# The second projection of a ConvFFN by half-block sums: seven products for eight, with two of four weight sums per pair by accumulating DMAs and two on VectorE

## The chip, the cores and the metric

One Trainium2 chip, one core. The metric is the device time of one launch in microseconds. The kernel before takes 1299.2 us (median of three runs, 1298.52 to 1301.49). Engines: TensorE (PE, with PEld for its weight loads), VectorE (DVE), ScalarE (ACT), GpSimd (POOL), SyncE (SP, which issues DMAs).

## The reference

Two decoder layers in float32, batch 1, 512 positions (S), width 1024 (D). Layer 0 mixes with gated linear attention (GLA), layer 1 with gated DeltaNet (GDN); each is followed by a ConvFFN, and each sublayer ends in a LayerNorm over `ALPHA * h + f(h)`.

```python
def conv_ffn(x, w_in, conv_w, w_out):
    h = causal_dwconv(x @ w_in, conv_w)          # 1024 -> 2 x 2816, then width 3 in time
    gate, up = jnp.split(h, 2, axis=-1)
    return (jax.nn.gelu(gate, approximate=False) * up) @ w_out   # 2816 -> 1024

def reference(x, ...):
    h = x
    for i in range(2):
        y = gla_mixer(h, ...) if i == 0 else gdn_mixer(h, ...)
        h = layer_norm(ALPHA * h + y, ln_g[i, 0], ln_b[i, 0])
        h = layer_norm(ALPHA * h + conv_ffn(h, ffn_w_in[i], ffn_conv_w[i], ffn_w_out[i]),
                       ln_g[i, 1], ln_b[i, 1])
    return h
```

The change touches the last product of `conv_ffn`, (512 x 2816) by (2816 x 1024), in both layers.

## The kernel before

Float32 products are made of three products of split operands: a value is cast to a high part (fp32r, on ScalarE) and the rest is its low part (a subtraction on VectorE), and PE adds high by high, low by high and high by low in one PSUM bank. `split_out` does that for activations, `issue` for weights: SP loads 512 KB into one of three `raw` buffers, ScalarE casts it to `wh` (L243), VectorE subtracts to `wl` (L244). There are four `wh`/`wl` buffers (`WB`). `prefetch` issues items of the list `plan` a little ahead of their use (`look`); `weight()` takes the next, `spend()` gives its buffer back. The last `TAIL` = 4 items of an FFN go, as 512-wide halves, into slots of the common pool of 53 (`wsh`, L233, and `wsl`, L234), so that they need no `wh` buffer.

An FFN has 22 blocks of 128 hidden channels (`f`). They are worked in two chunks, of 12 and 10. In a chunk, `fm_items` runs the up-projection: per block a gate item and an up item of 24 products 128 x 512 each, into a bank `fm`; then `ffn_conv` (one operation on ScalarE, two on VectorE, L643), a GELU on ScalarE, the product of both on VectorE (L658) and the split into `gh` and `gl` (L417, L418), laid out as 128 channels by 512 positions. After that `out_proj` runs the output projection for the chunk: for each half `hf` of the 1024 columns `tm_half` goes over pairs of K blocks, and for each over the four token blocks `tb`, each with a bank `tm` of its own; after the last pair `done` adds the bank to the residual `h[tb][hf]` (L379 in the first chunk, with ALPHA; L381 in the second), in the last chunk takes statistics (L386) and, when both halves of a token block are there, starts the LayerNorm generator. That one normalizes (L527 to L552), transposes on PE (`xT`, L166) and splits into `xh` and `xl` for the next stage, or, in the last layer, scales, shifts and stores the output (L593 to L595).

The order of each engine is set when the program is built: a scheduler gives every instruction its place by the written order and by costs that the kernel counts up (`clk`, `vec`), and the engine then takes its list in order. The lists shown under the change are those.

Of the kernel before, what the change touches and what calls it, by code (L numbers as in the profile page):

```python
# [9 lines left out]
F32R = mybir.dt.float32r  # L10
# [3 lines left out]
ALU = mybir.AluOpType  # L14

P = 128
D = 1024
S = 512
# [11 lines left out]
GDN_SCALE = 128.0 ** -0.5  # L30
CHUNKS = ((0, 12), (12, 22))
SLOTS = 53
# [16 lines left out]
def blk(i, n=P):  # L49
    return slice(i * n, i * n + n)  # L50


class Trunk:
# [3 lines left out]
    def __init__(self, ctx, tc):  # L57
# [23 lines left out]
        self.plan = []  # L81
        self.issued = 0
        self.taken = 0
        self.held = 0
# [64 lines left out]

    def mm(self, out, a, b, start=True, stop=True):  # L150
        n = 1
        for d in b.shape[1:]:
            n *= d
        self.clk += n * (0.00045 if b.dtype == F32R else 0.00175)
        t = self.nc.tensor.matmul(out, a, b, start=start, stop=stop)  # L155
        if self.pin:
            self.tc.keep_in_program_order(t)
# [40 lines left out]
    @staticmethod  # L198
    def in_slots(item):
        return item[0] == "tm" and item[5]  # L200

    def issue(self, item):

        nc = self.nc
        if item[0] == "rep":
            return self.issue_rep(*item[1:])
        used = 1024
        raw = self.raw if self.issued == 0 else self.rp.tile([P, 1024], F32, name=self.uid("raw"), tag="raw")
# [52 lines left out]

    def prefetch(self):
        while self.issued < min(len(self.plan), self.taken + self.look):
            item = self.plan[self.issued]
            if self.held == WB and not self.in_slots(item):
                break
            if self.after is None:
                self.ready.append(self.issue(item))
            else:
                with self.tc.issue_after(self.after):  # L270
                    self.ready.append(self.issue(item))
                self.after = None
            self.issued += 1

    def weight(self):
# [94 lines left out]
    def out_proj(self, a, n, first, final):  # L370
# [25 lines left out]
        self.look = LOOKAHEAD  # L396


    def exp_ln_table(self):
# [223 lines left out]
    def ffn_plan(self, w_in, w_out):  # L623
        for f0, f1 in CHUNKS:
            for f in range(f0, f1):
                self.plan_fm(w_in, f * P)
                self.plan_fm(w_in, DFF + f * P)
            self.plan_out(w_out, f0 * P, f1 - f0, TAIL if f1 == NF else 0)

# [16 lines left out]
    def ffn(self, cw, li, g, b, final, out=False):  # L646
        nc = self.nc
        for ci, (f0, f1) in enumerate(CHUNKS):
            gs, act, items = [], {}, []
            for f in range(f0, f1):  # L650
                def gate(ps, f=f):
                    a = self.ffn_conv(ps, cw, f)
                    nc.scalar.activation(a, a, AF.Gelu)  # L653
                    act[f] = a

                def up(ps, f=f):
                    u = self.ffn_conv(ps, cw, NF + f)
                    nc.vector.tensor_mul(u, u, act.pop(f))  # L658
                    t = self.slot("gh", F32R), self.slot("gl", F32R)
                    self.split_out(*t, u)  # L660
                    gs.append(t)

                items += [gate, up]
            self.fm_items(items)
            last = ci == len(CHUNKS) - 1
            if last:
                self.drain()
                self.ln_begin(li, g, b)
                if out:
                    self.ln_gb()  # L670
            a = lambda c, tb: (gs[c][0][:, blk(tb)], gs[c][1][:, blk(tb)])
            self.out_proj(a, f1 - f0, ci == 0, final if last else None)

# [694 lines left out]
```

## Time and profile before

| view | value |
|---|---|
| median of three runs | 1299.2 us (1298.52 to 1301.49) |
| profiled execution, span | 1300.2 us |
| PE busy | 1279.0 us, 98% |
| VectorE busy | 790.2 us, 61% |
| ScalarE busy | 546.8 us, 42% |
| GpSimd busy | 111.0 us, 9% |
| DMA, mean over the span | 97 GB/s, 126.52 MB |

The span is that of one execution taken by the profiler; it stands 1.0 us above the median of the runs. The shares are means over the whole span. In the page each of the 40 slices stands for 32.5 us; PE shows a 9 in nearly all of them, and the granted clock of PE a 9 in all but two, in the GDN mixer.

### The profile page before, as it was taken

The numbers are of one execution on the slowest core, as the hardware profiler recorded it, in microseconds if no ns is written. First come the engines' busy times: TensorE is split into PE (matmuls) and PEld (weight loads), VectorE is DVE, ScalarE is ACT, GpSimd is POOL, SyncE is SP. The second block draws the span as 40 slices with busy tenths as digits, with TensorE's granted clock in tenths as the row PEclk, the third lists the DMA queues.
The fourth block names the chain that finished last, engine by engine and source line by source line (L and its number), as shares of the span: only waits on it lengthen the run. The fifth ranks groups of instructions, "written<-read, shape, count | busy, mean of one in ns | idle before, by whom it ended". The sixth has DMA issues, their size and how long they took to land.

```text
span 1300.2 us, 17238 instructions
## 1 busy us (share of the span) xinstructions
PE 1279.0 (98%) x6666; PEld 1078.1 (83%) x6666; DVE 790.2 (61%) x1442; ACT 546.8 (42%) x1030; POOL 111.0 (9%) x150
## 2 busy tenths in 40 slices
PE   8999999999999999999999999999999999999996
PEld 6878888988888888889788889988888888888885
DVE  3673366676643466655799835669677653366656
ACT  3554443634421344425865535543554431244420
POOL 4000000070000000001111310100034000000000
PEclk9999999999999999999999968999999999999999
DMA  6421224143333333251543420333143333333331
GB/s 181 117 81 49 77 86 130 33 130 114 98 97 97 97 97 98 87 143 66 135 117 106 127 49 17 115 98 113 49 137 107 97 98 98 97 97 97 97 98 65
DMA packets 167089, 126.52 MB, mean 97 GB/s; under 512 B 16088, under 2 KB 139546, under 8 KB 167008
## 3 DMA queue, kind: packets, MB, share of 16 engines
q1 hardware_dynamic: 161728, 115.10, 30.0%
q0 software_dynamic: 3888, 8.50, 2.1%
q10 hardware_dynamic: 1392, 1.84, 0.4%
q8 instruction: 52, 0.85, 0.3%
q14 instruction: 29, 0.24, 0.1%
HBM read 119.63 MB, written 5.78 MB: 96 GB/s over the span
## 4 chain that ended last, share of the span: by engine, by line
PE 86%; issue 6%; DVE 5%; DMA 1%; ACT 1%; POOL 1%; DVEq 0%; POOLq 0%; ACTq 0%
PE fm L155 45%; PE tm L155 32%; PE o L155 1%; PE V L155 1%; PE R L155 1%; PE xT L166 1%; PE vn L155 1%; DVE ln_st L386 1%; PE pg L155 1%; PE yT L166 1%; PE qkT L166 1%; PE pq L155 0%; DMA gla_nw<-in_gla_norm_w_dram 0%; DVE wl L244 0%; DVE conv L940 0%
## 5 line engine op out<-in xcount | busy, mean ns | idle before, releaser
L244 DVE TENSOR_TENSOR wl<-raw,wh 128x1024 fp32r<-128x1024 f32 (+1 forms) x190 | 238.3, 1255 | 321.1 <-ACT wh L243 319.3
L155 PE MATMUL fm<-xh,wh 128*128 128x512 f32 (+1 forms) x1104 | 408.3, 370 | 0.4 <-ACT wh L243 0.4
L155 PE MATMUL fm<-xl,wh 128*128 128x512 f32 (+1 forms) x1104 | 404.8, 367 | 0.0
L155 PE MATMUL fm<-xh,wl 128*128 128x512 f32 (+1 forms) x1096 | 401.2, 367 | 2.5 <-DVE wl L244 2.5
L243 ACT CAST wh<-raw 128x1024 fp32r<-128x1024 f32 (+1 forms) x190 | 198.8, 1047 | 269.9 <-PE tm L155 159.4
L155 PEld LDWEIGHTS fm<-xh,wl 128*128 128x128 f32 x1096 | 207.4, 190 | 36.5 <-DVE wl L244 3.1
L155 PEld LDWEIGHTS fm<-xh,wh 128*128 128x128 f32 x1104 | 209.1, 189 | 34.2 <-ACT wh L243 1.2
L155 PEld LDWEIGHTS fm<-xl,wh 128*128 128x128 f32 x1104 | 209.3, 190 | 32.7
L643 DVE SCALAR_TENSOR_TENSOR conv<-fm,ffn_cw,conv 128x511 f32<-128x511 f32 (+1 forms) x176 | 130.7, 745 | 3.0
L155 PE MATMUL tm<-wl,gh 128*128 128x512 f32 x288 | 112.0, 389 | 0.0
L155 PE MATMUL tm<-wh,gh 128*128 128x512 f32 x288 | 112.0, 389 | 0.0
L155 PE MATMUL tm<-wh,gl 128*128 128x512 f32 x288 | 112.0, 389 | 0.0
L155 PE MATMUL tm<-wh,xh 128*128 128x512 f32 x192 | 79.5, 414 | 1.0 <-ACT qk L756 1.0
L417 ACT CAST gh<-conv 128x512 fp32r<-128x512 f32 x44 | 27.3, 621 | 124.7 <-DVE conv L658 124.6
L155 PE MATMUL tm<-wh,xl 128*128 128x512 f32 x192 | 75.4, 393 | 0.0
L155 PE MATMUL tm<-wl,xh 128*128 128x512 f32 x192 | 75.1, 391 | 0.0
L653 ACT ACTIVATE conv<-conv 128x512 f32<-128x512 f32 x44 | 27.8, 633 | 95.0 <-DVE conv L643 95.0
L155 PEld LDWEIGHTS tm<-wh,gh 128*128 128x128 f32 x288 | 54.1, 188 | 11.2
L155 PEld LDWEIGHTS tm<-wh,gl 128*128 128x128 f32 x288 | 54.1, 188 | 11.2
L155 PEld LDWEIGHTS tm<-wl,gh 128*128 128x128 f32 x288 | 54.1, 188 | 11.2
L641 ACT ACTIVATE conv<-fm,ffn_cw 128x512 f32<-128x512 f32 x88 | 59.9, 681 | 0.2
L940 DVE SCALAR_TENSOR_TENSOR conv<-fm,gdn_cw,conv 128x509 f32<-128x509 f32 (+2 forms) x72 | 53.2, 742 | 4.6 <-ACT conv L938 4.1
(274 smaller groups left out, 1555.4 us busy)
## 6 DMA issues: line engine op xcount, KB each, us to landing
raw<-in_ffn_w_in_dram SPq DMA_DIRECT2D x88, 512.0 KB, 3.7
raw<-in_ffn_w_out_dram SPq DMA_DIRECT2D x44, 512.0 KB, 3.7
raw<-in_gdn_w_in_dram SPq DMA_DIRECT2D x32, 512.0 KB, 4.0
raw<-in_gla_w_in_dram SPq DMA_DIRECT2D x23, 512.0 KB, 3.5
raw<-in_gla_w_out_dram SPq DMA_DIRECT2D x8, 512.0 KB, 3.5
raw<-in_gdn_w_out_dram SPq DMA_DIRECT2D x8, 512.0 KB, 3.8
hd<-h POOLq DMA_DIRECT2D x8, 256.0 KB, 2.5
dt<-drow POOLq DMA_DIRECT2D x8, 256.0 KB, 5.6
```

Of the source, the lines that this page charges most:

```text
L155: t = self.nc.tensor.matmul(out, a, b, start=start, stop=stop)
L166: t = self.nc.tensor.transpose(out, a, self.ident[:n, :n])
L243: nc.scalar.copy(wh[:, cols], raw[:, cols])
L244: nc.vector.tensor_sub(wl[:, cols], raw[:, cols], wh[:, cols])
L386: nc.vector.bn_stats(self.st[tb][:, hf, :], h)
L417: cast = self.nc.scalar.copy(dst_h, src)
L641: nc.scalar.activation(a, ps, AF.Identity, scale=tap(2))
L643: nc.vector.scalar_tensor_tensor(a[:, d:], ps[:, :S - d], tap(2 - d), a[:, d:], ALU.mult, ALU.add)
L653: nc.scalar.activation(a, a, AF.Gelu)
L940: self.conv = nc.vector.scalar_tensor_tensor(a[:, d:], ps[:, :S - d], tap(3 - d), a[:, d:], ALU.mult, ALU.add)
```

## The change

The output projection of a chunk is worked on 2 x 2 blocks, by a scheme of seven half-size products in place of eight. For a pair of K blocks (e, o), the activations are cut in two halves of 256 positions and the weights in two halves of 512 columns: activations x11, x21 (from e), x12, x22 (from o), weights q00, q01 (rows of e) and q10, q11 (rows of o). `combine` makes, once per pair on VectorE, the four sums s1 to s4 of activation halves, at half width, and splits them and x11, x12 and x22 into high and low parts. `plan_sums` makes the weight side in `wq` slots by quadrants of 256 KB: a and b are loaded by SP; b becomes q01 + q00 by an accumulating DMA from GpSimd (L221); c is loaded as q11, b += c on VectorE (L224); c becomes q11 + q01 by a second accumulating DMA; a is loaded anew as q10, and b += a on VectorE. Each of these values is split to high and low when its product comes (`split_duo`: ScalarE L276, VectorE L277).

`sums_proj` runs the products: three kinds of bank, A, B and C, two each (one per 128 positions of a half). Bank A collects x11, then s2 is added on top, then s3, then x22, and after each it is added to or subtracted from a block of `h` (`fold`, L506 in the first touch of a block, L508 later, and L511 for the statistics); B collects s1, then s4; C collects x12. There are 14 folds per chunk where there were eight. The chunks are three, of 6, 8 and 8 blocks. A pair takes 7 x 2 x 3 = 42 products, where before it took 2 x 4 x 2 x 3 = 48. PE has 5540 rows in its list for 5672, VectorE 1672 for 1342, GpSimd 186 for 142.

```diff
-CHUNKS = ((0, 12), (12, 22))
+PAIRS = ((0, 3), (3, 7), (7, 11))
+HALF = 2 * P
+AHEAD = 2
...
+    def plan_sums(self, w, rows, last):
...
+        def load(t, i, r, col):
+            t[i] = self.slot("wq")
+            nc.sync.dma_start(t[i], quad(i, r, col))
+        def add(t, i, r, col):
+            nc.gpsimd.dma_start(t[i], quad(i, r, col), accum_op=ALU.add)
+        def plus(t, i, u):
+            nc.vector.tensor_add(t[i], t[i], u[i])
...
+        for i in range(n):
+            duo([(a, i), (b, i)], -1, False, (load, a, i, 0, 0), (load, b, i, 0, 1), (add, b, i, 0, 0))
+        for i in range(n):
+            duo([(b, i), (c, i)], base + i, False, (load, c, i, 1, 1), (plus, b, i, c))
...
+        if last:
+            twos(a, load, 1, 0)
+            twos(c, add, 0, 1, slots=True)
+        else:
+            for i in range(n):
+                duo([(c, i), (a, i)], base + n + i, False, (add, c, i, 0, 1), (load, a, i, 1, 0))
+        twos(b, plus, a, slots=last)
...
+    def sums_proj(self, xs, first, final):
...
+        def prod(bank, i, which, w, j, end):
...
+            self.mm(ps, xh, w[0], begin, False, True)
+            self.mm(ps, xh, w[1], False, False, True)
+            self.mm(ps, xl, w[0], False, end, True)
+        def fold(bank, j, tb, hf, op, full):
...
+                nc.vector.tensor_tensor(h, h, banks[bank][j], op)
...
+        pairwise((("A", "x11"), ("B", "s1")),
+                 (lambda j: (j, 0, add, False), lambda j: (2 + j, 1, add, False)))
+        pairwise((("A", "s2"), ("B", "s4")),
+                 (lambda j: (j, 1, sub, False), lambda j: (j, 1, add, True)))
+        if final is None:
+            pairwise((("A", "s3"), ("C", "x12")),
+                     (lambda j: (2 + j, 1, sub, False), lambda j: (j, 0, add, False)))
+        else:
...                                      # C x12 (done(0), done(1)), then A s3, each over all pairs
+        ws = [x for k in range(0, n, 2) for x in self.weight()]
+        for j in range(2):
+            for i in range(n):
+                prod("A", i, "x22", ws[i], j, i == n - 1)
+            fold("A", j, 2 + j, 0, add, True)
+            done(2 + j)
...
+    def combine(self, e, o):
...
+        nc.vector.tensor_sub(r[:, t0], e[:, t1], o[:, t1])
+        nc.vector.tensor_sub(r[:, t1], r[:, t0], e[:, t0])
+        self.split_out(x11[:, t0], x11[:, t1], e[:, t0])
+        x |= halves(r, ("s1", "s2"))
+        nc.vector.tensor_sub(d[:, t0], e[:, t0], e[:, t1])
+        nc.vector.tensor_add(d[:, t1], o[:, t0], r[:, t1])
+        x |= halves(d, ("s3", "s4"))
+        x |= halves(o, ("x12", "x22"))
```

Three places show how the instructions stand. The first is PE at the end of FFN 1, where the last output products (`tm`), the transposes of the normalized residual (`xT`; `h_97` and `h_98` are the two column halves of token block 1, `h_99` and `h_100` of block 2, `h_101` and `h_102` of block 3) and the first products of the GDN mixer (`fm`, 256 positions wide) meet. Before:

```order
L155 MATMUL tm_4451<-wsh_4478,gh_4274 128x512
L155 MATMUL tm_4451<-wsl_4479,gh_4274 128x512
L155 MATMUL tm_4451<-wsh_4478,gl_4275 128x512
L166 MATMUL xT_4735<-ident_80,h_99 128x128 x4
L166 MATMUL xT_4784<-ident_80,h_100 128x128 x4
L155 MATMUL fm_4796<-xh,wh_4484 128x256
L155 MATMUL fm_4796<-xl,wh_4484 128x256
```

Now:

```order
L158 MATMUL tm_4636<-wsh_4863,gl_4628 128x512
L169 MATMUL xT_5038<-ident_80,h_97 128x128 x4
L169 MATMUL xT_5087<-ident_80,h_98 128x128 x4
L169 MATMUL xT_5101<-ident_80,h_99 128x128 x4
L169 MATMUL xT_5113<-ident_80,h_100 128x128 x4
L169 MATMUL xT_5127<-ident_80,h_101 128x128 x4
L158 MATMUL fm_5139<-xh,wh_4919 128x256
L158 MATMUL fm_5139<-xl,wh_4919 128x256
```

Before, two transposes stood between the last `tm` and the first `fm`, and those of `h_101` and `h_102` came later, among the `fm` products; now five stand there, that of `h_101` among them.

The second place is VectorE at the end of the last chunk of FFN 1 (`wl` of L244 and L326: splits of the GDN mixer's weights; `ln_`: steps of the LayerNorm of the token blocks that are done; `h_100<-h_100,tm`: the bank is added to the residual). Before:

```order
L569 TENSOR_TENSOR xl<-xf_4639,xh 128x4x128
L381 TENSOR_TENSOR h_100<-h_100,tm_4450 128x512
L386 BN_STATS ln_st_4437<-h_100 128x6
L527 BN_AGGR ln_mv_4668<-ln_st_4437 128x2
L529 TENSOR_SCALAR ln_var_4670<-ln_mv_4668 128x1
```

Now:

```order
L326 TENSOR_TENSOR wl_4920<-raw_4917,wh_4919 128x1024
L705 TENSOR_SCALAR ln_rs_4882<-ln_var_4880 128x1
L511 BN_STATS ln_st_4632<-h_97 128x6
L708 SCALAR_TENSOR_TENSOR ln_t_4883<-ln_rs_4882,ln_var_4880 128x1
L698 BN_AGGR ln_mv_4900<-ln_st_4632 128x2
L326 TENSOR_TENSOR wl_4926<-raw_4923,wh_4925 128x1024
L709 SCALAR_TENSOR_TENSOR ln_rs_4882<-ln_t_4883,ln_rs_4882 128x1
L700 TENSOR_SCALAR ln_var_4902<-ln_mv_4900 128x1
L326 TENSOR_TENSOR wl_4932<-raw_4929,wh_4931 128x1024
L708 SCALAR_TENSOR_TENSOR ln_t_4883<-ln_rs_4882,ln_var_4880 128x1
L705 TENSOR_SCALAR ln_rs_4904<-ln_var_4902 128x1
L508 TENSOR_TENSOR h_100<-h_100,tm_4635 128x512
```

The fold of `h_100` from bank A (`tm_4635`, which the products of x22 need next) now stands behind three weight splits and the LayerNorm steps of two token blocks.

The third place is VectorE in a middle stretch, where one sub-stage of output products gives way to the next. Before, between the two column halves of the first chunk:

```order
L379 SCALAR_TENSOR_TENSOR h_99<-h_99,tm_3144 128x512
L379 SCALAR_TENSOR_TENSOR h_101<-h_101,tm_3145 128x512
L244 TENSOR_TENSOR wl_3367<-raw_3364,wh_3366 128x1024
L244 TENSOR_TENSOR wl_3397<-raw_3394,wh_3396 128x1024
L244 TENSOR_TENSOR wl_3427<-raw_3424,wh_3426 128x1024
```

Now, in the middle chunk, from the second of the folds after x11 and s1:

```order
L508 TENSOR_TENSOR h_97<-h_97,tm_3652 128x512
L508 TENSOR_TENSOR h_100<-h_100,tm_3653 128x512
L224 TENSOR_TENSOR wq_3468<-wq_3468,wq_3657 128x512
L277 TENSOR_TENSOR wl_3689<-wq_3657,wh_3688 128x512
L224 TENSOR_TENSOR wq_3509<-wq_3509,wq_3659 128x512
L277 TENSOR_TENSOR wl_3689<-wq_3468,wh_3688 128x512
L277 TENSOR_TENSOR wl_3710<-wq_3659,wh_3709 128x512
L277 TENSOR_TENSOR wl_3710<-wq_3509,wh_3709 128x512
L224 TENSOR_TENSOR wq_3550<-wq_3550,wq_3667 128x512
L277 TENSOR_TENSOR wl_3732<-wq_3667,wh_3731 128x512
L508 TENSOR_TENSOR h_102<-h_102,tm_3654 128x512
L277 TENSOR_TENSOR wl_3732<-wq_3550,wh_3731 128x512
```

The four folds of a sub-stage, which stood together, now have sums and splits of weights between the third and the fourth.

151 lines of the change are left out of this document (135 added, 16 removed).

## The prediction

> **What bounds the kernel now.** I read the page first: the shares of the engines and the chain that ended last.
>
> ```profile
> span 1300.2 us, 17238 instructions
> PE 1279.0 (98%) x6666; PEld 1078.1 (83%) x6666; DVE 790.2 (61%) x1442; ACT 546.8 (42%) x1030; POOL 111.0 (9%) x150
> ...
> PE 86%; issue 6%; DVE 5%; DMA 1%; ACT 1%; POOL 1%; DVEq 0%; POOLq 0%; ACTq 0%
> ```
>
> TensorE is the bound, and VectorE has 39% of the span free. But shares are means, so next came the windows of the four parts of each ConvFFN (rows: its first up-projection, first output projection, second up-projection, second output projection with what follows; columns: width, then busy time of PE, PEld, DVE, ACT, POOL, then granted clock, DMA share, GB/s). I show the first FFN's and the last row of the second's.
>
> ```profile
> 241.10:367.90 126.80, 126.80 (x632) 108.07 (x631) 82.97 (x94) 55.45 (x79) 25.81 (x16) 1.00 0.34 104
> 367.90:433.20 65.30, 65.30 (x290) 54.08 (x289) 21.94 (x23) 13.71 (x14) 0.00 (x0) 1.00 0.32 97
> 433.20:542.00 108.80, 108.80 (x482) 90.09 (x481) 64.42 (x77) 44.23 (x59) 0.00 (x0) 1.00 0.33 97
> 542.00:599.20 57.20, 57.20 (x267) 47.48 (x266) 35.20 (x73) 22.80 (x40) 4.78 (x8) 1.00 0.42 121
> ...
> 1235.50:1300.20 64.70, 54.40 (x241) 44.72 (x239) 38.80 (x83) 8.54 (x13) 0.00 (x0) 0.96 0.24 82
> ```
>
> PE has no gap in the stages that change, apart from the very end. In the output projections VectorE is busy 21.94 of 65.30 us and 35.20 of 57.20. The chain in order of time gives PE's price and the two end points:
>
> ```profile
> 367.94 65.28 PE tm L155 x288
> 433.22 108.80 PE fm L155 x480
> 542.02 43.52 PE tm L155 x192
> ...
> 599.18 6.47 PE fm L155 x54
> ...
> 1235.50 38.09 PE tm L155 x168
> ```
> ```profile
> 1295.53 1.42 DVE L594 SCALAR_TENSOR_TENSOR h<-h,ln_rs,gb 128x512 f32<-128x512 f32 x2
> ```
>
> 65.28 us for 288 products is 226.7 ns each. After the last up-projection product of FFN 1 (542.0) the GDN mixer starts 57.2 us later; after that of FFN 2 (1235.5) VectorE's last operation ends 61.4 us later (1295.53 + 1.42, the second fence, from VectorE's order of time; the store of the output follows it in both kernels). I compare stages from such a point T.
>
> **What the change removes.** Per pair of K blocks 42 products stand for 48. 11 pairs in each FFN, two FFNs: 132 × 226.7 ns = 29.9 us of PE, 14.96 per FFN. This is the whole gain, and it is on the path as long as PE stays the bound.
>
> **What it adds to VectorE.** Its prices (groups: busy, mean ns of one, idle before):
>
> ```profile
> L244 DVE TENSOR_TENSOR wl<-raw,wh 128x1024 fp32r<-128x1024 f32 x188 | 237.0, 1261 | 319.9 <-ACT wh L243 318.0 <-DMA T<-dinvt 1.7
> L418 DVE TENSOR_TENSOR gl<-conv,gh 128x512 fp32r<-128x512 f32 x44 | 31.7, 721 | 29.0 <-ACT gh L417 29.0
> L234 DVE TENSOR_TENSOR wsl<-raw,wsh 128x512 fp32r<-128x512 f32 x32 | 20.7, 684 | 6.5 <-ACT wsh L233 6.5
> ```
>
> Alone, one 512-wide operation takes 0.68 us. In a row they overlap, as VectorE's order of time shows (start, time):
>
> ```profile
> 555.16 2.51 DVE L234 TENSOR_TENSOR wsl<-raw,wsh 128x512 fp32r<-128x512 f32 x4
> ...
> 566.34 1.28 DVE L381 TENSOR_TENSOR h<-h,tm 128x512 f32<-128x512 f32 x2
> 567.53 1.28 DVE L386 BATCH_NORM_STATS2 ln_st<-h 128x6 f32<-128x512 f32 x2
> 568.73 1.27 DVE L381 TENSOR_TENSOR h<-h,tm 128x512 f32<-128x512 f32 x2
> 569.91 1.28 DVE L386 BATCH_NORM_STATS2 ln_st<-h 128x6 f32<-128x512 f32 x2
> 571.11 1.21 DVE L244 TENSOR_TENSOR wl<-raw,wh 128x1024 fp32r<-128x1024 f32 x1
> ...
> 581.59 0.21 DVE L527 BATCH_NORM_AGGREGATE ln_mv<-ln_st 128x2 f32<-128x12 f32 x1
> ...
> 583.56 0.16 DVE L550 SCALAR_TENSOR_TENSOR ln_nb<-ln_mv,ln_rs 128x1 f32<-128x1 f32 x1
> 583.63 0.54 DVE L552 TENSOR_SCALAR h<-h,ln_mv,ln_rs 128x512 f32<-128x512 f32 x1
> ```
>
> From 566.34 to 571.11 stand eight operations in 4.77 us: 0.60 each. A 1024-wide one then costs some 1.15, and a small LayerNorm step about 0.2 (581.59 to 583.63: eleven). I take 0.60; the upper end is 0.69, the duration alone.
>
> *Up-projection stages.* `combine` takes away two 512-wide splits per pair and adds four half-width sums, one half-width and three full splits. With a half-width operation at 0.42 (between half of 0.60 and all of it) this is +2.7 us per pair of blocks. A pair lasts 21.8 us there (108.80 / 5) with 12.9 busy (64.42 / 5). It is hidden by VectorE's 8.9 free us; cost nothing, and without that cover 2.7 per pair. The cover ends at T: the last pair's `combine` runs into the sums.
>
> *Sums stages.* Per pair: seven 512-wide splits and two L224 sums are 9 × 0.60 = 5.4 us, per chunk 14 folds of 8.4 us. A chunk of four pairs (38.08 us of PE) then needs 36 + 14 = 50 operations, 30 us, plus the tail of `combine` of some 5; one of three pairs (28.56 us) 41, 24.6 us plus 5. VectorE goes from a third busy to nearly full, in one fixed order, so PE will wait wherever a fold or split stands behind something else.
>
> ScalarE and the queues first, since they have one answer.
>
> ```profile
> L233 ACT CAST wsh<-raw 128x512 fp32r<-128x512 f32 x32 | 18.2, 620 | 15.2 <-DMA raw<-in_gdn_w_out_dram 6.5 <-DMA raw<-in_ffn_w_out_dram 6.3 <-DMA raw<-in_gla_w_out_dram 2.4
> ```
>
> Seven casts per pair are 7 × 0.62 = 4.3 us of the 9.5 that its 42 products take: hidden by ScalarE's idle half; without that cover 4.3 per pair. SP issues four quadrant loads per pair for two item loads, and with the two accumulating ones 1.5 MB is fetched for 1.0. At a DMA share of 0.32 (windows) there is room; cost nothing, and if bandwidth were the limit half of a third of 38 us, 6 per chunk.
>
> Now the order of VectorE, chunk by chunk.
>
> - First chunk: VectorE needs 29.6 us against 28.56. I take 29.4, +0.8.
> - Middle chunk: banks of the first sub-stage are needed again in the second, and the fold h_102 stands at the end of eleven VectorE operations that begin with the first fold, at about T + 9.5 (42 of 48 products of that sub-stage): 9.5 + 12 × 0.60 = T + 16.7. PE wants bank B's second half at 48 + 20 products, T + 15.4. That is 1.3; with some 0.3 for the fold of h_100 ahead of it I take 39.7 against 38.08, +1.6.
> - Last chunk of FFN 1: from the fold at T + 9.5 to the fold of h_100, which frees bank A for the last product (x22), stand 43 512-wide operations, three 1024-wide GDN weight splits (L326) and nine small ones: 25.8 + 3.45 + 1.8 = 31.05, thus T + 40.6. PE could be there at T + 32.6 (144 products). It idles about 8 us before that, some 5 of them in one stretch at the end. Then 23 to 25 more operations of tokens 2 and 3 (three folds, four statistics, a weight split, LayerNorm, x splits) and their small steps, about 17 with what overlaps taken off at 16, end at T + 56.5; and in PE's order the transposes of tokens 2 and 3 stand ahead of GDN's first product, so after x22 (5.4 us, with waits near T + 48) PE idles a second time, some 8 us, and GDN starts at T + 57, where before it was T + 57.2 with two K blocks more.
> - Last chunk of FFN 2: no GDN weights. From T + 9.5, 50 operations of 0.60, 16 LayerNorm passes of 0.7 and the small ones that find no cover (4): 45.2, so T + 54.8, where before it was 61.4.
>
> **The sum.** FFN 1: 29.4 + 39.7 + 57.0 = 126.1 against 65.3 + 57.2 = 122.5: +3.6. FFN 2: 29.4 + 39.7 + 54.8 = 123.9 against 65.3 + 61.4 = 126.7: −2.8. Together +0.8. Two costs are not in it yet.
>
> *Accumulating DMAs.* 44 of them, on POOL's queue, none in the trace. Nearest rows (KB, us from issue to landing):
>
> ```profile
> raw<-in_ffn_w_out_dram SPq DMA_DIRECT2D x44, 512.0 KB, 3.7
> ...
> dt<-drow POOLq DMA_DIRECT2D x8, 256.0 KB, 5.6
> h<-hd POOLq DMA_DIRECT2D x8, 256.0 KB, 3.1
> ```
>
> Each waits for the plain load of its tile or for VectorE's reading of it; behind it waits ScalarE's cast, in order, and so PE. In the first chunk the later ones have some 3.5 us between that split and their use. At 3.1 they are free, at 5.6 each FFN pays about 2 us there, and if they need 8 about 5. They add besides fetching, so I stand between 3.1 and 5.6, nearer the upper: +1 per FFN, +2 in all. Less than nothing is excluded: no load is saved.
>
> *The clock.* An idle stretch of PE has a follower in this trace (windows around the GDN's wait for a DMA):
>
> ```profile
> 742.80 3.45 DMA rm<-dinv
> ```
> ```profile
> 740.00:745.00 5.00, 3.86 (x63) 3.04 (x61) 2.81 (x4) 2.04 (x3) 4.46 (x9) 1.00 0.68 163
> 745.00:750.00 5.00, 4.40 (x53) 4.00 (x48) 1.53 (x6) 1.93 (x9) 4.83 (x9) 0.57 0.40 67
> 750.00:755.00 5.00, 5.00 (x51) 4.46 (x50) 1.63 (x4) 1.63 (x3) 0.63 (x1) 0.50 0.29 46
> ```
>
> The granted clock falls to 0.57 and 0.50 in the ten us after a wait of 3.45. Ten us at half clock lose 5. In FFN 1's last chunk I expect idle stretches of about 5 and 8 us. The first is followed by work that waits for VectorE anyway, so only the second can cost, up to 5; I take 3. The bounds are 0 and 10. [...]
>
> In all 0.8 + 2 + 3 = +5.8 on a span of 1300.2, so 1306.0; the median of the three runs is 1299.2, 1.0 below the profiled execution, which gives **1305**.
>
> **Rivals.**
> 1. *The gain stays* (opposite sign). In favour: VectorE's need (30 of 38 us) is below PE's in each chunk, and PE can run ahead inside a sub-stage. Against: the last chunk's count, which needs no estimate of a DMA. If x22 finds its bank at T + 34 rather than 40.6 and GDN's first products run before tokens 2 and 3 are done, only a third to a half of the 29.9 is lost: 1280 to 1290. With no stall at all 1270. The point where it decides: the mean spacing of VectorE in the sums. At 0.50 the last chunk is 4.3 us shorter in FFN 1 and 5 in FFN 2, and the sum is below the time before.
> 2. *The adds land late.* At 8 us or more they hold ScalarE and VectorE, which take work in order; 5 per FFN in the first chunk and some 3 in each of the others: +22 rather than +2, 1315 to 1325. Against: POOL's queue has only these DMAs there, and DMA share is 0.32.
> 3. *VectorE costs 0.69.* At 684 ns per operation rather than 0.60 the last chunks grow by 43 × 0.084 = 3.6 and 50 × 0.084 = 4.2, the others by some 2 each: 1317. The timeline above speaks against it where nothing waits, but a wait between two operations takes the overlap away. [...]
> 4. *No change*: the two FFNs cancel and the clock stays up: 1297 to 1302.
>
> **How the numbers follow.** ±0.2% (2.6 us) is about what a measurement of this kernel can tell from no change. My forecast (1302 to 1312) has 0.38, rivals 2 and 3 together (1312 to 1325) 0.22, no change 0.13, the gain that stays 0.27. Faster is 0.27, same 0.13, slower 0.60. The range of eight in ten leaves out the better part of rival 1 (0.12) and the top of 2 (0.06): 1285 to 1321. Since both signs hold much of the chance, the likeliest case's own range is 1302 to 1312.
>
> **What the profile after would show.** Right: VectorE near 90% busy in the sums stages; PE idle of 5 to 8 us in FFN 1's last chunk, released by L508 on VectorE; GDN's first product about 57 us after the last up-projection product; a clock below 1.00 there; 462 products per FFN in the sums. Wrong: PE gapless through the sums (rival 1); PE waits released by ScalarE's L276 behind a DMA, and L221 landing in 8 us (rival 2); VectorE's spacing 0.68 in series (rival 3). My weakest step is the hand count of the last chunks: it assumes that VectorE never idles from T + 9.5, and that its order is the one in which PE needs the results.

## The result and the profile after

The changed kernel takes 1310.7 us (median of six runs, 1304.8 to 1314.6) where the kernel before takes 1300.5 in the same comparison: ratio 1.008, 95% interval 1.0057 to 1.0102. It is slower by 10.2 us, in the direction forecast and inside the range; the forecast was 1305. The profiled execution has a span of 1308.3 us, 8.1 more than that of before.

Page of the changed kernel, first lines and the chain:

```profile
span 1308.3 us, 17669 instructions
PE 1259.7 (96%) x6534; PEld 1054.9 (81%) x6534; DVE 934.8 (71%) x1772; ACT 603.9 (46%) x1176; POOL 146.4 (11%) x194
...
PE 67%; DVE 16%; issue 10%; DMA 3%; ACT 3%; POOL 1%; SPq 0%; DVEq 0%; POOLq 0%; ACTq 0%
```

PE did lose 132 products (6666 to 6534), and its busy time 19 us of the 29.9; the products that met a halved clock last longer (in x22 of FFN 1, at 0.50, one took 0.43 us for 0.23). VectorE stands in the chain with 16% where it had 5%. The windows show where (columns as in the prediction; the rows are the three sums stages of FFN 1, then of FFN 2, each from its first product of the sums, the point T of the prediction, to the first product of what follows; the last row ends with VectorE's last operation):

```profile
302.70:339.70 37.00, 33.44 (x132) 26.42 (x131) 32.28 (x54) 15.74 (x26) 2.54 (x3) 0.91 0.21 42
425.60:466.20 40.60, 39.19 (x170) 31.46 (x169) 34.65 (x57) 18.36 (x30) 3.41 (x4) 1.00 0.27 56
553.10:610.00 56.90, 45.56 (x198) 36.09 (x197) 52.52 (x119) 31.33 (x60) 9.04 (x14) 0.92 0.32 81
1002.10:1038.00 35.90, 32.34 (x132) 25.25 (x131) 32.23 (x53) 15.78 (x27) 2.59 (x3) 0.95 0.22 42
1124.00:1163.60 39.60, 38.77 (x170) 31.45 (x169) 34.54 (x57) 18.30 (x30) 3.46 (x4) 1.00 0.26 57
1250.50:1305.30 54.80, 39.68 (x169) 30.96 (x167) 51.53 (x115) 15.00 (x27) 3.45 (x4) 0.93 0.28 72
```

VectorE is busy 85 to 94% of each stage. The first chunk of each FFN contains 0.91 us (four products) of the next up-projection, which is taken off where chunks are compared. The forecast for these rows, in turn: 29.4, 39.7, 57.0, 29.4, 39.7, 54.8. The four later stages came to within a microsecond of the hand count; both first chunks are 5.6 to 6.7 us longer than it.

The stages sum to 263.0 us without the 0.91s, 13.8 more than the 249.2 of before. The span grew by 8.1 only, since the GDN mixer between the FFNs, which the change does not touch, was shorter in this execution (before, then after):

```profile
599.00:934.60 335.60, 331.94 (x2170) 286.88 (x2169) 243.38 (x615) 176.76 (x472) 39.61 (x75) 0.95 0.32 91
```
```profile
609.90:940.70 330.80, 327.64 (x2165) 283.89 (x2165) 239.03 (x599) 173.53 (x466) 38.88 (x74) 0.97 0.32 93
```

4.8 us less at a granted clock of 0.97 for 0.95. Of the experiments below, number 11 had 326.5 at 0.98, number 2 had 329.4 at 0.97 and number 5, which changes only when this mixer's weights are issued, 335.3 at 0.95. So the length goes with the clock of the single execution. Stage lengths are therefore read inside the FFNs, and times from the medians.

What PE waited for, longest groups:

```profile
PE tm L158 <- DVE ln_rs L709: 5.0, 1, 5.0
PE tm L158 <- DVE gx L589: 4.1, 2, 2.0
PE xT L169 <- DVE ln_var L700: 3.0, 1, 3.0
```

The first and the third are the end of FFN 1 (in the first, the view names L709, the small step that stands next to the fold of `h_100` in VectorE's list), the second is the last pair's `combine` in the two first chunks.

### The profile page after: what moved, and what is told of

It reads as the page before. It is cut to its first block, busy times and chain, and to the rows that moved or that the text cites. A ratio compares the mean times of both kernels' runs of the same rounds, so it can differ in the third digit from the quotient of the medians.

```text
span 1308.3 us, 17669 instructions
## 1 busy us (share of the span) xinstructions
PE 1259.7 (96%) x6534; PEld 1054.9 (81%) x6534; DVE 934.8 (71%) x1772; ACT 603.9 (46%) x1176; POOL 146.4 (11%) x194
## 4 chain that ended last, share of the span: by engine, by line
PE 67%; DVE 16%; issue 10%; DMA 3%; ACT 3%; POOL 1%; SPq 0%; DVEq 0%; POOLq 0%; ACTq 0%
PE fm L158 38%; PE tm L158 20%; DMA wq<-in_ffn_w_out_dram 2%; PE o L158 1%; DVE wl L277 1%; DVE conv L814 1%; DVE wl L326 1%; DVE h L508 1%; DVE gl L589 1%; PE R L158 1%; DVE wq L224 1%; PE V L158 1%; DVE conv L1135 1%; ACT wh L276 1%; DVE ln_st L511 1%
## 5 line engine op out<-in xcount | busy, mean ns | idle before, releaser
L326 DVE TENSOR_TENSOR wl<-raw,wh 128x1024 fp32r<-128x1024 f32 (+1 forms) x154 | 188.3, 1225 | 201.4 <-ACT wh L325 199.5
L325 ACT CAST wh<-raw 128x1024 fp32r<-128x1024 f32 (+1 forms) x154 | 160.8, 1046 | 258.6 <-PE fm L158 153.7
L814 DVE SCALAR_TENSOR_TENSOR conv<-fm,ffn_cw,conv 128x511 f32<-128x511 f32 (+1 forms) x176 | 131.0, 745 | 5.8 <-ACT conv L812 3.4
L276 ACT CAST wh<-wq 128x512 fp32r<-128x512 f32 x138 | 80.5, 618 | 69.4 <-DVE wq L224 34.0
L277 DVE TENSOR_TENSOR wl<-wq,wh 128x512 fp32r<-128x512 f32 x138 | 90.4, 683 | 21.8 <-ACT wh L276 21.4
L221 POOL DMA_DIRECT2D wq<-in_ffn_w_out_dram x44 | 37.9, 908 | 513.9 <-DMA wq<-in_ffn_w_out_dram 356.9
L158 PE MATMUL tm<-wh,gh 128*128 128x512 f32 x232 | 89.4, 399 | 5.3 <-ACT wh L276 2.4
L158 PE MATMUL tm<-wl,gh 128*128 128x512 f32 x232 | 92.0, 396 | 2.1 <-DVE wl L277 2.1
L158 PE MATMUL tm<-wh,gl 128*128 128x512 f32 x232 | 90.8, 394 | 0.0
L754 POOL TENSOR_TENSOR h<-h,gb 128x512 f32<-128x512 f32 x16 | 25.7, 1631 | 299.6 <-DMA gb<-in_ln_g_dram 299.6
L158 PEld LDWEIGHTS tm<-wh,gh 128*128 128x128 f32 x232 | 44.2, 191 | 18.5 <-ACT wh L276 3.4
```

The source lines that it names most:

```text
L158: t = self.nc.tensor.matmul(out, a, b, start=start, stop=stop, skip_group_check=open_group)
L221: nc.gpsimd.dma_start(t[i], quad(i, r, col), accum_op=ALU.add)
L276: nc.scalar.copy(wh, t[i])
L277: nc.vector.tensor_sub(wl, t[i], wh)
L325: nc.scalar.copy(wh[:, cols], raw[:, cols])
L326: nc.vector.tensor_sub(wl[:, cols], raw[:, cols], wh[:, cols])
```

## The experiments

**1. The chunking alone.** In the kernel before:

```diff
-CHUNKS = ((0, 12), (12, 22))
+CHUNKS = ((0, 6), (6, 14), (14, 22))
```

> The kernel before, with eight products per pair, but worked in three chunks of 6, 8 and 8 blocks instead of two of 12 and 10. It does the chunking of the change alone. If VectorE's load in the sums is what costs, this kernel stays within 2.6 us of the kernel before (1300.5): its folds are 24 for 16 per FFN, 8 x 0.60 = 4.8 us more on a VectorE that is a third busy there. If the chunking itself costs (a third change of stage per FFN, 12 blocks less of cover), it is 4 to 8 us slower than before, and the half-block sums are cleared of that part.

Measured: 1300.5 us, ratio to before 1.0003 (0.9977 to 1.0028). Three chunks cost nothing that this run could show. Its windows also give what each chunk takes with eight products (first, middle and last chunk of FFN 1, last of FFN 2; the first and middle chunks of FFN 2 take as long as those of FFN 1):

```profile
302.20:335.00 32.80, 32.80 (x146) 27.17 (x145) 14.59 (x17) 8.05 (x9) 0.00 (x0) 1.00 0.37 111
421.90:465.60 43.70, 43.70 (x194) 36.22 (x193) 17.04 (x19) 9.61 (x10) 0.00 (x0) 1.00 0.32 97
552.40:598.70 46.30, 46.30 (x218) 38.41 (x217) 32.14 (x71) 20.35 (x37) 4.77 (x8) 1.00 0.41 117
1243.70:1294.40 50.70, 43.68 (x193) 35.85 (x191) 36.33 (x81) 6.50 (x11) 0.00 (x0) 0.98 0.22 73
```

Against these the half-block sums lose 3.3 and 2.2 us in the first chunks, gain 3.1 and 4.1 in the middle ones, and lose 10.6 and 4.1 in the last: 13.0 us in all. The question is no longer whether the sums pay, but where.

**2. Four sums by accumulating DMAs.**

```diff
-            duo([(b, i), (c, i)], base + i, False, (load, c, i, 1, 1), (plus, b, i, c))
+            duo([(b, i), (c, i)], base + i, False, (load, c, i, 1, 1), (add, b, i, 1, 1))
...
-        twos(b, plus, a, slots=last)
+        twos(b, add, 1, 0, slots=last)
```

> The changed kernel with all four weight sums per pair by accumulating DMAs: the two that VectorE made (L224) become two more accumulating DMAs, 44 operations of VectorE less in all, 88 accumulating DMAs for 44. If VectorE is the bound in the sums (theory A), eight operations less ahead of the last fold of each last chunk are 4.8 us: GDN starts at T + 52 for 56.9, FFN 2 ends at T + 49 for 53.0, and with some 1 us in the other chunks the time falls by 8 to 11 us, to 1300 to 1303. If the accumulating DMAs are the bound (theory B; 4.8 us from issue to landing, 0.9 of GpSimd each, and each must wait for the split of its tile and be waited for by the next), PE waits longer for ScalarE's casts behind them and the time rises by 3 to 12 us, to 1314 to 1323.

Measured: 1326.9 us, 1.0206 (1.0172 to 1.024), 16 us slower than the changed kernel. The middle chunks, in which nothing else stands, show it (FFN 1, FFN 2):

```profile
426.20:471.90 45.70, 40.84 (x170) 32.43 (x169) 30.08 (x49) 18.14 (x30) 8.19 (x10) 0.96 0.52 98
1129.00:1176.30 47.30, 42.02 (x170) 33.64 (x169) 30.19 (x49) 18.36 (x30) 7.98 (x10) 0.93 0.48 92
```

VectorE is relieved (30.1 us for 34.6) and the stage still grows by 5.1 and 7.7: theory B holds for this version, and the time lies even beyond its 1314 to 1323. ScalarE's casts wait for these tiles 49.5 us in all, where in the changed kernel it is 18.9. The issue lines of the changed kernel give the time from issue to landing:

```profile
wq<-in_ffn_w_out_dram POOLq DMA_DIRECT2D x44, 256.0 KB, 4.8
```

With 88 of them it is 5.2. Plain transfers of 256 KB on the same queue took 3.1 to 5.7 us in the changed kernel, and the plain loads of the same tiles by SP 5.5, so the adding itself has no price that these rows show. What costs is the chain: each add must wait for the split that reads its tile, and a cast must wait for the add. Whether the fuller queues (a DMA share of 0.52 for 0.27) cost besides was not separated.

**3. Four sums on VectorE**, none by DMA (b += a while a is still q00; later c = b - a):

```diff
-            duo([(a, i), (b, i)], -1, False, (load, a, i, 0, 0), (load, b, i, 0, 1), (add, b, i, 0, 0))
+            duo([(a, i), (b, i)], -1, False, (load, a, i, 0, 0), (load, b, i, 0, 1), (plus, b, i, a))
...
+        def renew(t, i, r, col):
+            nc.vector.tensor_sub(c[i], b[i], a[i])
+            load(t, i, r, col)
```

> The changed kernel with all four weight sums on VectorE and no accumulating DMA: b += a (a still being q00), later c = b - a, which is q11 + q01. VectorE gets 44 operations more, GpSimd's 44 DMAs and their 11.5 MB go. The runs before showed that four sums by DMA cost 16 us (1326.9). If VectorE is the bound (theory A), eight operations more ahead of the last folds of each last chunk are 4.8 us there and 1 to 2 in the other chunks: 1319 to 1325. If the chains from VectorE's split over the accumulating DMA (4.8 us) to ScalarE's cast are what costs (theory B), they go and the time falls to 1302 to 1307. If both cost alike: 1309 to 1314.

Measured: 1319.7 us, 1.0163 (1.0133 to 1.0193), 9 us slower than the changed kernel: theory A. But the place differs from the expectation. First chunks of FFN 1 and 2:

```profile
302.70:342.40 39.70, 33.90 (x135) 26.64 (x134) 35.70 (x59) 15.60 (x26) 0.00 (x0) 0.91 0.08 23
1003.30:1043.00 39.70, 33.61 (x135) 26.32 (x134) 35.77 (x59) 15.57 (x26) 0.00 (x0) 0.91 0.07 21
```

They are 2.7 and 3.8 us longer than in the changed kernel, of which 0.7 each is three more products of the next up-projection. The middle chunks grew by 0.6 and 1.5, the last ones by 0.2 and 1.2 only, not 4.8: in the last chunk of FFN 1 four of the eight operations added fall before T, into VectorE's free time of the up-projection. ScalarE's waits for these tiles, 18.9 us in the changed kernel, fall to 3.1. With both sums moved either way the kernel gets slower; of the three ways that were run, two and two is the fastest.

**4. Dummy products where PE idles:** 10 before the last pair of the first chunks and 24 ahead of x22 in FFN 1.

```diff
+        def warm(count, which, w):
+            for _ in range(count):
+                self.nc.tensor.matmul(banks["C"][0], xs[0][which][0][:, blk(0)], w, start=True, stop=True)
```

> The changed kernel with 44 products more that nobody reads, on a bank that is free, at the places where PE idles: 10 ahead of the last pair of the first chunk in each FFN, 24 ahead of x22 in FFN 1's last chunk, 10.0 us of PE in all. They fill idle time and keep PE busy. If the halved clock after the idle stretches costs, the granted clock stays at 1.00 through the sums and the time falls by 3 to 6 us, to about 1305 to 1308. If VectorE sets the pace in any case and the halved clock is hidden by its waits, the time stays at 1309 to 1312; if the filling products are late themselves, 1311 to 1316.

Measured: 1309.1 us, 1.0074 (1.0045 to 1.0102), not told apart from the changed kernel. The end of FFN 1:

```profile
552.80:608.30 55.50, 48.83 (x221) 39.73 (x220) 51.01 (x117) 29.83 (x55) 9.00 (x14) 0.96 0.32 80
```

5.4 us of products that nobody needs were put into this stage, and it is 1.4 us shorter, not longer. PE's time is free there; VectorE sets when x22 can start. The clock did not stay at 1.00 (0.95 in both first chunks, 0.96 here, where it fell later, after a wait of 4.9 us ahead of the last transposes), so the run is no clean answer on it. For the first chunks another pair gives one: in experiment 7 they ran at 1.00 and took as long (36.9 and 36.1) as in the changed kernel at 0.91 and 0.95 (37.0 and 35.9). There the halved clock lay under the waits. At the end of FFN 1 it did not; see the part on the prediction.

**5. GDN's weights issued later.**

```diff
-        while self.issued < min(len(self.plan), self.taken + self.look):
+        while self.issued < min(len(self.plan), self.taken + self.look, self.cap):
...                        # cap: the plan's items of this FFN, lifted once x22's first half is written
```

> The changed kernel, in which the GDN mixer's weights are not issued before the first half of x22 is written: the fold of h_100 then stands ahead of four weight splits (L326) on VectorE in place of behind three of them. The same work in another order. Theory A: PE's wait of 5.0 us ahead of x22 goes nearly, but VectorE has the same list to get through before tokens 2 and 3 are transposed, so GDN starts at T + 55.5 to 57 as before (56.9), and the time stays at 1308 to 1312. Rival: the order is what costs; GDN starts at T + 52, and the time falls to 1304 to 1307.

Measured: 1309.8 us, 1.0094 (1.0059 to 1.0129): no change. The wait of 5 us ahead of x22 went, and GDN started at T + 54.8 for 56.9:

```profile
554.80:609.60 54.80, 44.36 (x197) 35.03 (x196) 50.90 (x117) 30.36 (x58) 8.60 (x13) 0.93 0.31 74
```

Of the 5 us 2 came through. The rest turned into a longer wait for the LayerNorm of tokens 2 and 3 (6.2 us ahead of a transpose, where the longest there was 3.0). That is theory A in kind, though 0.7 us below its 55.5, and far from the rival's T + 52.

**6. GpSimd's residual step earlier.** The first chunks were still unexplained. In the changed kernel's VectorE list, before and during GpSimd's scale and shift of the residual (L754, L755, 272.5 to 296.9 us):

```profile
263.91 0.43 DVE L856 TENSOR_TENSOR gr<-conv,conv 128x256 f32<-128x256 f32 x1
...
283.88 1.52 DVE L814 SCALAR_TENSOR_TENSOR conv<-fm,ffn_cw,conv 128x511 f32<-128x511 f32 x2
285.44 1.48 DVE L829 TENSOR_TENSOR conv<-conv,conv 128x512 f32<-128x512 f32 x1
286.95 1.40 DVE L856 TENSOR_TENSOR gr<-conv,conv 128x256 f32<-128x256 f32 x1
```

The operations shown with two inputs in SBUF take 1.4 to 1.5 us for 0.42 or 0.69 (others in this stretch less: full-width splits 1.01); the one that reads PSUM (L814, two in 1.52; ahead of the step, at 261.56, two in 1.53) is not slowed. GpSimd's operation lasts as long:

```profile
285.08 2.98 POOL L754 TENSOR_TENSOR h<-h,gb 128x512 f32<-128x512 f32 x2
```

1.49 each. Why the one slows the other no row shows; that the slowing goes with the step is seen by moving it, as here, and by leaving it out (experiment 8).

```diff
-RESID_DELAY = 24.0
+RESID_DELAY = 4.0
```

> The changed kernel with RESID_DELAY 4 for 24: GpSimd's scale and shift of the residual (L754, L755) is started some 20 us earlier in the up-projection before the first sums of each FFN. Theory A: in the trace of the changed kernel VectorE's operations between SBUF tiles take 1.4 us for 0.42 (128x256) while GpSimd runs these, so VectorE comes late to the last pair's combine, PE waits 0.79 + 2.03 us and its clock falls to 0.61; moved away, the first chunk's products (302.7 to 339.7, 0.9 of it other work) last 30 to 32 us for 36.0, in both FFNs, and the time falls by 7 to 11 us to 1300 to 1304. Theory B: the first chunk is long because the accumulating DMAs land late; then it stays at 35 to 36 us and the time at 1309 to 1312.

Measured: 1322.8 us, 1.0182 (1.0152 to 1.0212), 12 us slower than the changed kernel: the expected time was wrong. The steps now ran at 226 to 256 us, under the LayerNorm ahead of the FFN, on VectorE:

```profile
231.42 1.25 DVE L708 SCALAR_TENSOR_TENSOR ln_t<-ln_rs,ln_var 128x1 f32<-128x1 f32 x1
232.70 1.21 DVE L709 SCALAR_TENSOR_TENSOR ln_rs<-ln_t,ln_rs 128x1 f32<-128x1 f32 x1
```

Steps of one element that take 0.15 to 0.22 elsewhere take 1.2. The first chunks, however, shrank, to 33.7 and 30.4 us (34.6 and 31.3 with the 0.91):

```profile
313.90:348.50 34.60, 31.59 (x132) 23.94 (x131) 30.02 (x50) 14.55 (x25) 2.54 (x3) 1.00 0.21 41
1020.40:1051.70 31.30, 30.55 (x132) 24.22 (x132) 27.93 (x46) 13.78 (x23) 2.59 (x3) 1.00 0.22 44
```

**7. A delay between the two,** 14 for 24:

> The changed kernel with RESID_DELAY 14 for 24. With 4 the GpSimd operations ran at 226 to 256 us, in the LayerNorm ahead of the FFN, whose small VectorE steps took 1.2 us for 0.2, and the kernel took 1322.8. With 24 they run at 272 to 297, shortly before the first sums. If there is a place between, after the LayerNorm (it ends at about 250) and well before the sums (302), the first chunks come to 30 to 33 us and the time falls to 1301 to 1306. If the operations still meet the LayerNorm, 1312 to 1322.

Measured: 1312.4 us, 1.0117 (1.0092 to 1.0143). It moved nothing: the steps ran at 274.7 to 299.0 us, released by the landing of their scale rows, not by the delay. Inconclusive for its question, but its first chunks answer the one on the clock:

```profile
304.70:341.60 36.90, 31.85 (x132) 23.87 (x131) 32.39 (x54) 15.68 (x26) 2.54 (x3) 1.00 0.21 42
1004.40:1040.50 36.10, 31.94 (x133) 23.89 (x131) 32.37 (x55) 16.54 (x28) 2.59 (x3) 1.00 0.23 45
```

**8. Without GpSimd's residual step.** The scale and shift of the residual are left out; nothing else, so the output is not the layer's.

```diff
-            nc.gpsimd.tensor_mul(h[hf], h[hf], gb[hf])
-            nc.gpsimd.tensor_add(h[hf], h[hf], gb[2 + hf])
```

> The changed kernel without the scale and shift of the residual on GpSimd (L754, L755) after the mixers' LayerNorms: 16 operations of about 1.5 us per FFN are left out, nothing else is moved. The run with these some 20 us earlier cut the first chunk's products in FFN 2 from 35.0 to 30.4 us but collided with the LayerNorm before. If GpSimd's slowing of VectorE is what made the first chunk late, both first chunks come to 30 to 31.5 us (36.0 and 35.0 before; 28.6 is PE alone), no half clock there, and the time falls by 8 to 11 us, to 1300 to 1303. If the accumulating DMAs set the first chunk, it stays above 34 us and the time at 1308 to 1312.

Measured: 1301.9 us, 1.0023 (1.0002 to 1.0043). First chunks of FFN 1 and 2:

```profile
302.60:337.30 34.70, 32.33 (x132) 25.42 (x131) 28.15 (x47) 13.96 (x23) 2.54 (x3) 0.95 0.21 43
998.30:1029.80 31.50, 30.58 (x132) 24.28 (x131) 28.03 (x46) 13.85 (x23) 2.54 (x3) 1.00 0.22 45
```

Without the 0.91, 30.6 us in FFN 2, near the hand count (29.4), and 33.8 in FFN 1: the step costs 4.4 us in FFN 2 and 2.3 in FFN 1.

The run alone leaves a rival. GpSimd takes its list in order, and in the changed kernel the first three accumulating DMAs of FFN 1 stand directly behind the residual step, at 296.87 us; here the first is issued at 289.81. So the step could also have cost by holding up the adds. The chain of the changed kernel (start, time, what) speaks against it:

```profile
286.95 1.40 DVE gr L856
288.34 1.43 DVE gx L589
...
321.10 4.89 DMA wq<-in_ffn_w_out_dram
```

It goes into the first sums through VectorE's slowed operations, in FFN 2 likewise, and the first add on it is the one of 321.10, at the change to the last sub-stage. In the kernel without the step an add is on the chain into FFN 1's sums (issued at 293.25, 7.4 us to landing), none into FFN 2's: in FFN 1 the adds are the next limit, which is why less came back there. What stays besides is a wait of 2.1 us at the change to the last sub-stage, behind the cast of the chunk's last add.

**9. Chunks of 4, 4 and 3 pairs.**

```diff
-PAIRS = ((0, 3), (3, 7), (7, 11))
+PAIRS = ((0, 4), (4, 8), (8, 11))
```

> The changed kernel with chunks of 4, 4 and 3 pairs for 3, 4 and 4. The first chunk's losses (35 and 36.1 us for 28.6 of PE) came of VectorE's late combine of the last pair, which three pairs do not cover, and the last chunk's of VectorE's list. Theory A: the first chunk of four pairs takes 39.5 to 41 us (as the middle one, 40.7 and 39.8), so 4 to 5 us more for 9.5 of PE; the last one of three pairs has 9 operations of VectorE less per pair, 5.4 us: GDN starts at T + 51 for 56.6, FFN 2 ends at T + 49 for 54.8. Together 1 to 3 us less: 1306 to 1310. If the last chunk follows PE instead (9.5 us less each), 1298 to 1302.

Measured: 1312.6 us, 1.0108 (1.0074 to 1.0143). The first chunk and the last of FFN 1:

```profile
326.40:372.00 45.60, 40.83 (x170) 32.42 (x169) 38.61 (x63) 21.35 (x37) 3.39 (x4) 0.96 0.34 82
563.60:611.20 47.60, 35.83 (x160) 28.41 (x159) 44.72 (x107) 25.91 (x49) 8.39 (x13) 0.91 0.34 87
```

The last stage fell to 47.6, by 9.3 us, which is not theory A's T + 51 but nearly the 9.5 of PE that the other case named. The first took 45.6, 5 to 6 more than a middle chunk of the same size. ScalarE's list at its start, in the next kernel, which has the same first chunk (T = 324.8):

```profile
324.79 1.14 ACT L276 CAST wh<-wq 128x512 fp32r<-128x512 f32 x2 [4.03 <-DMA wq<-in_ffn_w_out_dram]
...
328.79 0.62 ACT L276 CAST wh<-wq 128x512 fp32r<-128x512 f32 x1 [1.40 <-DMA wq<-in_ffn_w_out_dram]
...
330.36 0.68 ACT L815 ACTIVATE conv<-fm,ffn_cw 128x512 f32<-128x512 f32 x1
```

Here the casts that wait for the accumulating DMAs stand ahead of the last block's convolution, which comes 5.5 us after T. In the middle chunk of the changed kernel that convolution comes 0.5 us after T. GpSimd issued the first of these adds 7.2 us ahead of T (317.57), in that middle chunk 13.4 us (412.23 for 425.6). So theory A missed for the first chunk: with four pairs it is the adds that are late. What held them back was not tested.

**10. Eight products in the last chunk, sums in the first two,** with 4, 4, 3 pairs and with 3, 4, 4.

```diff
-            self.plan_sums(w_out, range(2 * p0, 2 * p1, 2), 2 * p1 == NF)
+            if 2 * p1 == NF:
+                self.plan_out(w_out, 2 * p0 * P, 2 * (p1 - p0), min(TAIL, p1 - p0))
+            else:
+                self.plan_sums(w_out, range(2 * p0, 2 * p1, 2), False)
```

> Chunks of 4, 4 and 3 pairs; the half-block sums in the first two, and in the last chunk the eight products of the kernel before, with the activations split per block. Theory A: where four pairs run without the LayerNorm behind them, the sums cost 39.7 to 40.7 us for the 43.5 of eight products (192 x 226.7 ns), so 3 to 4 us are kept in each of four chunks, and the last chunk ends as before the change, with PE never idle: 1300 less 11 to 15 us, 1285 to 1289. Rival: GpSimd's slowing of VectorE hits the first chunk again (then 43 us and more), and two chunks give 6 to 8: 1292 to 1294. If the change costs by itself, wherever it stands, 1298 to 1304.

> The same with chunks of 3, 4 and 4 pairs: the sums in the first two, eight products in the last. The first chunk of three pairs takes 35 to 36 us with sums and would take 32.6 with eight products (144 x 226.7 ns): a loss of 2.5 to 3.5 per FFN; the middle one gains 3 to 4. So 1298 to 1302, no faster than the kernel before, and the difference to the kernel with 4, 4 and 3 is what the size of the first chunk is worth.

Measured: 1302.1 us, 1.0022 (0.9997 to 1.0046), for 4, 4, 3: theory A missed by 13 us, and the time is beyond the rival's 1292 to 1294 too, in the range of the third case. The first chunk took 46.2, which is the rival's "43 us and more", but behind the late adds of experiment 9; GpSimd's residual step was over at 298 us, 27 before T. 1296.8 us, 0.9982 (0.9957 to 1.0008), for 3, 4, 4: 1 us below the range and, as expected, no difference that can be told from before.

**11. Sums in the middle chunk alone** (3, 4, 4 pairs; the first and last chunk as in the kernel before):

```diff
-            if 2 * p1 == NF:
+            if p0 == 0 or 2 * p1 == NF:
```

> Chunks of 3, 4 and 4 pairs; half-block sums in the middle chunk alone, eight products in the first and the last. By the stages measured so far: the middle chunk takes 39.7 to 40.7 us with sums for 43.75 with eight products, and the first and last chunks stay as in the kernel with three chunks and eight products (32.9 and 46.2 or 50.7 us), which takes 1300.5. So 3.1 and 4.0 us less: 1292 to 1294.5, faster than both kernels. If the stage times do not add up that way (the next stages wait for what VectorE has left over), 1297 to 1301.

Measured: 1288.8 us, ratio to before 0.9912 (0.9886 to 0.9937): faster than both kernels, and 3 us below the expected range. The middle chunks of FFN 1 and 2, and the last of FFN 1:

```profile
422.70:462.40 39.70, 38.87 (x170) 31.52 (x170) 34.55 (x57) 18.36 (x30) 3.38 (x4) 1.00 0.27 57
549.30:595.50 46.20, 46.20 (x217) 38.35 (x216) 32.12 (x70) 20.27 (x37) 4.76 (x8) 1.00 0.41 117
1103.50:1143.20 39.70, 38.87 (x170) 31.52 (x170) 34.55 (x57) 18.47 (x30) 3.43 (x4) 1.00 0.28 60
```

4.0 us less than eight products in each middle chunk, and nothing lost in the others. By stages that is 8 us; the median fell by 11.3 against its own runs of the kernel before. The lower end of that interval is 8.2 us (1300.1 × 0.0063), so the stages explain what is certain; the other 3 us stay open.

## Why the prediction was right, and where it was not

- *The gain.* 132 products went, as counted, and PE was idle or waiting in their place in four of the six stages.
- *The last chunk of FFN 1.* The fold of `h_100` was to end at T + 40.6. In VectorE's list it stands behind the three weight splits, and ends 40.4 us after T = 553.1:

```profile
588.23 1.21 DVE L326 TENSOR_TENSOR wl<-raw,wh 128x1024 fp32r<-128x1024 f32 x1
...
592.81 0.68 DVE L508 TENSOR_TENSOR h<-h,tm 128x512 f32<-128x512 f32 x1
```

  GDN started at T + 56.9 for 57 predicted. Counting VectorE's list between two events, at 0.60 each, was enough for both points. PE's side was less exact: it waited 5.0 us ahead of x22, as predicted, but then 3.0 and 1.2 ahead of the transposes and not 8, because x22 itself ran for 4 us at half clock (0.50 from 593.5 to 597.5). That the transposes gate GDN's first product held; experiment 5 shows that the order of the splits is worth 2 us of the 10.6 that the stage loses.
- *The last chunk of FFN 2* ended at T + 54.8, as predicted. The term was compared with a two-chunk stage (61.4), which hid that eight products in the same chunk end at 50.7; the sum was right, the reading that FFN 2 gains there was not.
- *The middle chunks:* 40.6 and 39.6 us for 39.7. The fold of `h_102` ended at T + 16.5, for 16.7 counted, but the wait of 1.3 us that was expected behind it did not come; PE waited 0.2 us for another fold, 0.6 for a weight split and, in FFN 1, 0.6 for a later fold. So the size is right in part by luck.
- *The first chunks* are the term that failed: 36.1 and 35.0 for 29.4 (its own count of VectorE gave 29.6, which changes nothing). The working put VectorE's list from T on and took "+2.7 per pair" as covered by the up-projection's 8.9 free microseconds. That cover was not there when the last pair but one was combined: GpSimd's residual step lay over it, from 272.5 to 296.9 us of an up-projection that ends at 302.7, and made VectorE's half-width sums last three times as long. The trace of before had it, in rows that I did not compare:

```profile
286.08 1.47 DVE L658 TENSOR_TENSOR conv<-conv,conv 128x512 f32<-128x512 f32 x1
...
297.71 0.69 DVE L658 TENSOR_TENSOR conv<-conv,conv 128x512 f32<-128x512 f32 x1
```

  Leaving the step out gave 4.4 us back in FFN 2 and 2.3 in FFN 1 (experiment 8). ScalarE's part is seen in the changed kernel's list: the last block's convolution ran 4.8 us after T = 302.7, behind casts that waited for DMAs and for VectorE (without the residual step it ran 0.6 us after T):

```profile
302.76 0.63 ACT L276 CAST wh<-wq 128x512 fp32r<-128x512 f32 x1 [0.32 <-DMA wq<-in_ffn_w_out_dram]
304.08 0.62 ACT L276 CAST wh<-wq 128x512 fp32r<-128x512 f32 x1 [0.69 <-DMA wq<-in_ffn_w_out_dram]
...
307.04 0.62 ACT L276 CAST wh<-wq 128x512 fp32r<-128x512 f32 x1 [0.56 <-DVE wq L224]
307.56 0.68 ACT L812 ACTIVATE conv<-fm,ffn_cw 128x512 f32<-128x512 f32 x1
```

- *The accumulating DMAs* land in 4.8 us by the median, between the bounds of 3.1 and 5.6, nearer the upper as taken; single ones took longer (7.4 in experiment 8). That they hurt where they are late (the mechanism of rival 2) is shown by experiment 2 and, in the first chunk, by 9.
- *The clock* was priced at +3, for the stretch after the second idle time. Its premise was a misreading: the 3.45 us in the trace of before are the time of a DMA on the chain, while PE itself waited 0.65, 0.49 and 0.60 us there, with small products between, so that case does not show what an idle stretch of that length does. The effect came all the same. At the start of GDN PE had no gap, and got through 26 products in one five-us stretch and 44 in the next:

```profile
610.00:615.00 5.00, 5.00 (x26) 5.00 (x25) 2.21 (x4) 4.54 (x12) 0.20 (x1) 0.51 0.28 105
615.00:620.00 5.00, 5.00 (x44) 5.00 (x43) 0.29 (x1) 0.00 (x0) 0.00 (x0) 1.00 0.00 0
```

  That is 2 us lost, on the chain that ended last, where before the clock was 1.00 (44 products in five us). So the term was near its size. In the first chunks, where no price was set, the clock also fell (to 0.61, after waits of 0.79 and 2.03 us), but at no cost: in experiment 7 the same waits, 0.90 and 2.04, left it at 1.00, and the chunks were equally long.
- *Rival 1*, the gain that stays, is true of the middle chunks alone, by 3 to 4 us each. *Rival 3* fell: five splits in a row took 3.09 us.
- *The sum:* +5.8 forecast; +13.8 in the stages of the profile, +10.2 in the medians. The first chunks are 12.3 of the 13.0 that the stage terms missed. Of the 5 that were added for DMAs and clock, some 2 came, at GDN's start; the rest makes up for part of the first chunks, in the wrong place. That the time lies within the range is owed in part to that, and so to luck.

## What to carry to other kernels

When an edit trades TensorE products for VectorE operations, count VectorE's list in each stage between two events of the critical engine, and make the trade only in stages where that list ends first: here the middle chunks gave 4 us each, and the gain was lost again where a LayerNorm followed, where GpSimd ran beside VectorE, or where the weight sums came late. Free time of VectorE was no cover here where GpSimd's scale and shift of the residual ran in it (1.40 to 1.51 us for 0.42, four sums and a split at half width); compare the durations of one VectorE operation inside and outside GpSimd's busy slices before relying on it. When work can go to a loaded engine or to a queue, try the split as well: here two sums each way was faster (1310.7 us) than four either way (1326.9 and 1319.7).

## What the runs showed of the hardware

- VectorE operations with two SBUF inputs took longer beside a GpSimd operation of 1.49 us: 1.40 to 1.51 us for 0.42 (128x256), 1.01 to 1.53 for 0.69 (128x512), 1.4 to 2.3 for 1.2 (128x1024) and, in experiment 6, 1.2 for 0.2 (128x1). The small ones lose most. The one that reads PSUM there (L814, 128x511) did not change: two in 1.52 us beside it, 1.53 ahead of it.
- An accumulating DMA of 256 KB took 4.8 us to land, and with 88 of them for 44 5.2; plain ones of that size on the same queue took 3.1 to 5.7.
- The GDN mixer, the same products in each kernel, took between 326 and 336 us from one profiled execution to the next, the longer the lower its granted clock, from 0.98 to 0.95:

```profile
595.50:922.00 326.50, 323.33 (x2167) 280.30 (x2165) 243.10 (x615) 176.13 (x471) 39.65 (x75) 0.98 0.33 95
```

  This is the kernel of experiment 11; two others stand in the section on the result. In the kernel before, whose instructions do not change, the runs beside experiment 3 went from 1293.5 us at a granted clock of 0.994 to 1304.6 at 0.984. So a single span is no measure of an edit of a few us.
